# Attention with the latent heads' fifth score product and the meta keys' value product at full height

## The chip, the cores and the metric

The kernel runs on one core of a Trainium2 chip. The metric is the device time of one execution in microseconds (us). A core has TensorE (PE, matrix products, with its weight loads listed apart as PEld), VectorE (DVE), ScalarE (ACT), GpSimd (POOL) and SyncE (SP), which here issues most DMAs. Matrix products read two operands from SBUF, one held in the array (the weights) and one streamed, and add into PSUM.

## What is computed

Two transformer blocks run on 2048 tokens. The change is in the attention of the second one, which puts 16 meta tokens ahead of the 2048 (so L = 2064 keys) and has two kinds of heads:

```
q_m = concat([q[..., :NOPE_DIM], rotate(q[..., NOPE_DIM:])])        # 4 latent heads, 128 + 64 wide
k_m = concat([kv[..., :NOPE_DIM], broadcast(k_rot)])                # the 64 rotated columns are shared
o_mla = attend(q_m, k_m, v_m, QK_DIM ** -0.5)
o_gqa = attend(qg, kg, vg, GQA_DIM ** -0.5)                         # 4 grouped heads on 2 key heads, 128 wide
```

`attend` is softmax(q k^T * scale) v over all 2064 keys. The outputs of the meta queries are not needed.

## The kernel before

**Precision.** Operands of matrix products are split in two parts, high and low, each held as fp32r; a product of two split operands is made of three (high x high, high x low, low x high), added up in PSUM.

**Stages.** The kernel runs one stage after the other: first block, projections of the second (`GqaKeys.early` and `late` start loads of keys and values at the end of it), attention (`phase_d`), output projection and routing, experts. In the trace attention lies between about 1392 and 2670 us.

**Units.** Attention is 64 units, each one head and 256 queries (`QT`): 32 of the grouped heads (`hd` 4 to 7) and then 32 of the latent heads (`hd` 0 to 3). A unit has two halves `j` of 128 queries. Its steps are methods of `Unit`:

- `q(j, g)`: the scores of 128 queries against key group g (512, 400 or three times 384 keys; ten such calls in a unit). A grouped head takes three products (L1308 to L1310). A latent head takes two more for the 64 rotated columns (L1312, L1313). `qr` holds high and low part of the rotated query on top of each other, 64 partitions each; `kT[0][:, 1]` and `kT[1][:, 1]` hold the high and the low part of the rotated key, each written twice, on partitions 0 to 63 and 64 to 127. So L1312 makes (high + low query) x high key in one product, and L1313 the high query x low key on 64 partitions. After each group DVE takes the row maximum (L1314).
- `e(j, g)`: exp on ACT into `P`. After group 1 POOL copies the 16 meta columns three times beside themselves (L1329).
- `t(p)`: four transposes of `P` into PSUM (L1344), and a split by ACT (`ph`, L67) and DVE (`pl`, L68).
- `h(p)`, `l(p)`: value products with the high and low part of the weights of softmax (L1367), four and two.
- `m`, `a`: the same for the meta keys. `m` transposes four copies of the 16 columns (L1351); ACT copies them to `pm`, and DVE turns the lower 32 partitions into the low part. `a` is one value product with 64 partitions of `pm` against 64 of the value tile (`vc[0]` or `gk.v[0]`, block `NT`), where the DMAs of `META_ROWS` put high and low values in the matching order.
- `f`: the last step of a unit.

**Order.** Within attention the order is written out by hand in `ORDERS` (a latent unit plays `ORDERS[1]`): `n` is the next unit, `c` the current, `p` the previous one; `nq04` is `q(0, 4)` of the next unit, `ca` is `a` of the current. Every engine takes its part of this list in order. `ORDERS[1]` reads:

```
"nq00 ct1 ce13 nq01 ce12 ch0 pf ct2 ce14 cl0 ch1 nq02 nq03 nq04 ct3 cl1 ch2 ne02 ct4 ne01 ne00 ne03 "
"cl2 ch3 ne04 nq10 ct5 nq13 cl3 ct6 nq11 nq12 nq14 ch4 ct7 ch5 ne10 cl5 cm cl4 ne11 cl6 ch7 ch6 cl7 "
"ca nt0"
```

In `ORDERS[0]`, for grouped heads, the end is `nt0 ca cl7`. Scores have five PSUM buffers (`psS`), transposes two (`psT`), sums of values one (`psA`).

Of the kernel before, what the change touches and what calls it, by code (L numbers as in the profile page):

```python
# [8 lines left out]
F32 = mybir.dt.float32  # L9
F32R = mybir.dt.float32r  # L10
# [3 lines left out]
OP = mybir.AluOpType  # L14
# [7 lines left out]
NT = S // 128  # L22
# [782 lines left out]


def phase_c(cx, a, h, dr, mix, early, late):
    tc, nc = cx.tc, cx.nc
    es, ez, er = ExitStack(), ExitStack(), ExitStack()
# [40 lines left out]
    with es, tc.manual_schedule():  # L850
# [311 lines left out]
        t3 = cx.pool(es, "ct3")  # L1162
        pending += queries(NT - 1, t3)
        early()
        stats(NT)
        for n_, f in enumerate(pending):
# [12 lines left out]
QT = 256  # L1179
# [11 lines left out]
     "cl2 ch3 ne04 nq10 ct5 nq13 cl3 ct6 nq11 nq12 nq14 ch4 ct7 ch5 ne10 cl5 cm cl4 ne11 cl6 ch7 ch6 cl7 "  # L1191
     "ca nt0"))
META_ROWS = ((0, 32), (16, 48))


META_PART = ((S, L),)
# [3 lines left out]
def load_keys(nc, dst, src, parts=WHOLE):  # L1200
    for c0, c1 in parts:
        at = META_AT if c0 == S else c0 if c0 < META_AT else c0 + N_META
        nc.sync.dma_start(dst[:, at:at + c1 - c0].bitcast(F32), src[:, c0:c1])


class GqaKeys:
# [4 lines left out]
    def early(self):  # L1211
        nc, dr = self.cx.nc, self.dr
        c = self.cx.pool(self.es, "dg", side="right")
        self.kT = [c.tile([128, 2, L], F32R, name=f"kg{z}") for z in range(2)]
        self.v = [c.tile([128, KT, 256], F32R, name=f"vg{z}") for z in range(2)]
        self.q0 = c.tile([128, 2, QT], F32R, name="q0")
        nc.sync.dma_start(self.q0.bitcast(F32), dr["qg"][:, :, 0, :QT])
        for part in KEY_PARTS[:2]:
            for z in range(2):
                load_keys(self.cx.nc, self.kT[z][:, 0, :], self.dr["kT"][:, z, 0, :], [part])  # L1220

    def values(self, z, b):
        nc, src, bs = self.cx.nc, self.dr["v"], slice(b * 128, (b + 1) * 128)
        nc.sync.dma_start(self.v[z][:, :NT, bs].bitcast(F32), src[z, :S, bs].rearrange("(k p) d -> p k d", p=128))
        for p0 in META_ROWS[z]:
            nc.sync.dma_start(self.v[0][p0:p0 + N_META, NT, bs].bitcast(F32), src[z, S:, bs])
# [9 lines left out]


def phase_d(cx, a, dr, o, gk, after_gqa, first):
    tc, nc = cx.tc, cx.nc
    mm = nc.tensor.matmul  # L1240
    es = ExitStack()
    with es, tc.tile_pool(name="ds", bufs=5, space=PSUM) as psS, \
            tc.tile_pool(name="dp", bufs=2, space=PSUM) as psT, \
            tc.tile_pool(name="da", bufs=1, space=PSUM) as psA:
        t_ = cx.pool(es, "dt", 2)
        c = cx.pool(es, "dc")
        kT = [c.tile([128, 2, L], F32R, name=f"kT{z}") for z in range(2)]
        vc = [c.tile([128, KT, 128], F32R, name=f"vc{z}") for z in range(2)]
        wv = [c.tile([128, 4, 128], F32R, name=f"wv{z}") for z in range(2)]
        wvr = t_.tile([128, 4, 128], F32, name="wvr", bufs=1)  # L1250

        def load_k(z, b):
            load_keys(nc, kT[z][:, b, :], dr["kT"][:, z, 2 + b, :])

        def load_v(z):
            nc.sync.dma_start(vc[z][:, :NT, :].bitcast(F32), dr["c"][z, :S, :].rearrange("(k p) d -> p k d", p=128))
            for p0 in META_ROWS[z]:
                nc.sync.dma_start(vc[0][p0:p0 + N_META, NT, :].bitcast(F32), dr["c"][z, S:, :])
# [12 lines left out]
        def load_q(u):  # L1271
            qc, hd = place(u)
            ts = slice(qc * QT, (qc + 1) * QT)
            if u == 0:
                return gk.q0, None
            q = t_.tile([128, 2, QT], F32R, name="q", bufs=3)
            src = dr["qm"] if hd < 4 else dr["qg"]
            nc.sync.dma_start(q.bitcast(F32), src[:, :, hd % 4, ts])
            qr = None
            if hd < 4:  # L1280
                qr = t_.tile([128, QT], F32R, name="qr", bufs=3)
                nc.sync.dma_start(qr.bitcast(F32), dr["qr"][:, hd, ts])
            return q, qr
# [3 lines left out]
        class Unit:  # L1287
# [10 lines left out]
            def q(self, j, g, last=NG - 1):  # L1298
                if len(self.P) == j:
                    self.mx.append(cx.c.tile([128, 8], F32, name="mx", bufs=4))  # L1300
                    self.P.append(t_.tile([128, L + 3 * N_META], F32, name="P", bufs=4))
                js = slice(j * 128, (j + 1) * 128)
                kt = kT if self.mla else gk.kT
                b = 0 if self.mla else (self.hd - 4) // 2
                gs = slice(*GROUPS[g])
                po = psS.tile([128, 512], F32, name="S")[:, :gs.stop - gs.start]
                q, qr = self.qs, self.qr
                mm(po, q[:, 0, js], kt[0][:, b, gs], start=True, stop=False)  # L1308
                mm(po, q[:, 0, js], kt[1][:, b, gs], start=False, stop=False)
                mm(po, q[:, 1, js], kt[0][:, b, gs], start=False, stop=not self.mla)  # L1310
                if self.mla:
                    mm(po, qr[:, js], kT[0][:, 1, gs], start=False, stop=False)  # L1312
                    mm(po, qr[:64, js], kT[1][:64, 1, gs], start=False, stop=True)  # L1313
                nc.vector.tensor_reduce(self.mx[j][:, g:g + 1], po, AX.X, OP.max)  # L1314
                self.sg[j, g] = po
                if g == last:
                    nm = cx.c.tile([128, 1], F32, name="nm", bufs=4)
                    nc.vector.tensor_reduce(nm, self.mx[j][:, :NG], AX.X, OP.max)
                    nc.vector.tensor_scalar(nm, nm, -self.scale, None, op0=OP.mult)  # L1319
                    self.nm.append(nm)  # L1320
                    self.sm.append(cx.c.tile([128, 8], F32, name="sm", bufs=4))
# [26 lines left out]
            def m(self):  # L1348
                ps = psT.tile([128, 2, QT], F32, name="T")[:64, 0, :]
                for j in range(2):  # L1350
                    nc.tensor.transpose(ps[:, j * 128:(j + 1) * 128], self.P[j][:, META_AT:META_AT + 4 * N_META],  # L1351
                                        cx.ident)
                self.pm = t_.tile([64, QT], F32R, name="pm")
                nc.scalar.copy(self.pm, ps)
                nc.vector.tensor_tensor(self.pm[32:], ps[32:], self.pm[32:].bitcast(F32), OP.subtract)

            def val(self, k, z):
                if self.mla:
# [26 lines left out]
                    self.add(2 * p + i, 0, self.pp[p][1][:, i, :])  # L1385

            def a(self):
                self.add(NT, 0, self.pm, 64)

            def f(self):  # L1390
                ps = psT.tile([128, 2, QT], F32, name="T")
# [507 lines left out]
def phase_g(cx, a, h1, acc, tables, olist, out):  # L1899
# [4 lines left out]
    with es, tc.tile_pool(name="gp", bufs=4, space=PSUM) as pj, \  # L1904
# [23 lines left out]
        class Slot:  # L1928
# [142 lines left out]
            def down(self, cs, get, begin, end, feed):  # L2071
# [16 lines left out]
                for j in range(self.nt if early else 0):  # L2088
                    open_[j] = (pd if j < 2 else pj).tile([128, 512], F32, name="pd" if j < 2 else "pj")
                    self.product(open_[j], j, ws, range(early))  # L2090
# [345 lines left out]
def block_kernel(tc, a, out):  # L2436
    cx = Ctx(tc)
    with tc.tile_pool(name="scratch", bufs=1, space=DRAM) as dp:
        def scratch(name, shape, dt=F32):
            return dp.tile(list(shape), dt, name=name)  # L2440

        hT = scratch("hT", (128, 10, S))
        h = scratch("h", (L, D))
        dr = {"v": scratch("dr_v", (2, L, 256)), "c": scratch("dr_c", (2, L, 128)),
              "kT": scratch("dr_kT", (128, 2, 4, L)), "qg": scratch("dr_qg", (128, 2, 4, S)),
              "qm": scratch("dr_qm", (128, 2, 4, S)), "qr": scratch("dr_qr", (128, 4, S))}
        o = scratch("o", (S, D))
        h1 = scratch("h1", (ROWS, D))
        acc = scratch("acc", (ROWS, D))
        tables = [scratch(f"table{k}", (NE * STRIDE, 2)) for k in range(TOPK)]  # L2450
        olist = scratch("olist", (DUMP, 2), I32)
        mix = MixOut(cx, a, hT, h)
        phase_a(cx, a, hT, mix.ahead)
        gk = GqaKeys(cx, a, dr)
        phase_c(cx, a, h, dr, mix, gk.early, gk.late)
        op = OutProj(cx, a)
        phase_d(cx, a, dr, o, gk, op.load, partial(op.first, o))
        phase_f(cx, a, op, o, h, h1, acc, tables, out)
        phase_g(cx, a, h1, acc, tables, olist, out)
        cx.close()  # L2460
# [55 lines left out]
```

## Time and profile before

| | |
|---|---|
| runs | 5524.70, 5524.92, 5529.76 us; median 5524.92 us |
| profiled execution | span 5522.8 us from its first to its last instruction |
| busy over the span | PE 96%, weight loads 87%, DVE 68%, ACT 49%, POOL 29% |
| granted TensorE clock over the span | 0.984 of full speed |

The profile gives no time of its own for the profiled execution beside the span. The median of the runs is 2.1 us above the span. A row of the timeline has the start of an instruction (or of several alike in a row, with their number at the end) and how long it took; the time from one start to the next is what the engine needs for the first of them.

### The profile page before, as it was taken

How to read it: one execution, taken by the hardware profiler on the slowest of the kernel's cores; microseconds unless marked ns; L12 is line 12 of the kernel's file. 1: busy time of each engine (PE TensorE's matmuls, PEld its weight loads, DVE VectorE, ACT ScalarE, POOL GpSimd, SP SyncE). 2: the span in 40 equal slices, each digit the busy share in tenths (PEclk: the TensorE clock that was granted, in tenths of full speed). 3: DMA queues.
4: the chain of work that ended last, by engine and by line, in shares of the span. 5: the costliest groups of instructions: out<-in, count | busy, mean ns of one | idle time of the engine just before them, and what ended most of it. 6: DMA issues, size and time to landing. Idle time of an engine off the chain costs nothing. (4 is left out here: it accounts for less than half of the span.)

```text
span 5522.8 us, 89101 instructions
## 1 busy us (share of the span) xinstructions
PE 5316.3 (96%) x33672; PEld 4777.8 (87%) x33672; DVE 3734.1 (68%) x6827; ACT 2689.6 (49%) x5404; POOL 1605.8 (29%) x1567
## 2 busy tenths in 40 slices
PE   8999999899999999999997999999999999999997
PEld 7888878687899977777776999999999999998886
DVE  6787768544787755555697755766667667777758
ACT  4443433333677644445433544455555545555553
POOL 1232137555000021000343322233333233323327
PEclk9999999999999999999998999999999999999998
DMA  4333344344410110000335655666666666767675
GB/s 129 115 111 100 92 151 155 111 145 144 121 52 27 31 46 25 22 24 31 129 123 155 211 153 168 194 185 183 196 194 197 191 200 196 212 193 206 201 211 183
DMA packets 733017, 761.08 MB, mean 138 GB/s; under 512 B 109700, under 2 KB 673870, under 8 KB 732582
## 3 DMA queue, kind: packets, MB, share of 16 engines
q1 hardware_dynamic: 702768, 678.51, 39.3%
q0 software_dynamic: 27776, 74.33, 5.6%
q8 instruction: 267, 4.37, 0.3%
q10 hardware_dynamic: 2038, 2.48, 0.1%
q14 instruction: 168, 1.38, 0.1%
HBM read 626.35 MB, written 128.84 MB: 137 GB/s over the span
## 5 line engine op out<-in xcount | busy, mean ns | idle before, releaser
L68 DVE TENSOR_TENSOR wlo<-raw,whi 128x1024 fp32r<-128x1024 f32 (+1 forms) x751 | 923.7, 1240 | 433.1 <-ACT whi L67 423.3
L67 ACT CAST whi<-raw 128x1024 fp32r<-128x1024 f32 (+1 forms) x1000 | 960.8, 987 | 481.6 <-PE pj L73 166.2
L68 POOL TENSOR_TENSOR wlo<-raw,whi 128x1024 fp32r<-128x1024 f32 (+1 forms) x249 | 552.9, 2221 | 1705.0 <-ACT whi L67 1525.6
L72 PE MATMUL pj<-xsA,whi 128*128 128x256 f32 (+11 forms) x1792 | 593.5, 331 | 19.5 <-ACT g L2038 9.5
L73 PE MATMUL pj<-xsA,whi 128*128 128x256 f32 (+11 forms) x1792 | 590.8, 330 | 0.3 <-DVE xsA L68 0.3
L74 PE MATMUL pj<-xsA,wlo 128*128 128x256 f32 (+11 forms) x1792 | 589.3, 329 | 0.0
L67 ACT CAST ph<-T 128x512 fp32r<-128x512 f32 x512 | 300.4, 587 | 503.6 <-PE T L1344 496.9
L68 DVE TENSOR_TENSOR pl<-T,ph 128x512 fp32r<-128x512 f32 x512 | 353.5, 691 | 206.0 <-ACT ph L67 203.5
L2011 PE MATMUL pj<-xsB,whi 128*128 128x312 f32 (+11 forms) x1664 | 483.5, 360 | 4.3 <-DVE g L2041 4.3
L1314 DVE TENSOR_REDUCE mx<-S 128x1 f32<-128x384 f32 (+2 forms) x640 | 360.8, 581 | 95.1 <-PE S L1313 94.6
L2013 PE MATMUL pj<-xsB,wlo 128*128 128x156 f32 (+11 forms) x1664 | 418.2, 251 | 0.0
L72 PE MATMUL pd<-whi,atA 128*128 128x256 f32 (+4 forms) x1360 | 395.2, 291 | 17.4 <-ACT atA L67 15.0
L73 PE MATMUL pd<-wlo,atA 128*128 128x256 f32 (+4 forms) x1360 | 384.0, 282 | 8.1 <-POOL wlo L68 7.0
L74 PE MATMUL pd<-whi,atA 128*128 128x256 f32 (+4 forms) x1360 | 384.6, 283 | 3.8 <-DVE atA L68 3.5
L1325 ACT ACTIVATE P<-S,nm 128x384 f32<-128x384 f32 (+2 forms) x640 | 384.3, 609 | 7.2 <-DVE nm L1319 4.0
L1329 POOL COPY P<-P 128x48 f32<-128x48 f32 x128 | 28.5, 223 | 1176.9 <-ACT P L1325 1163.2
L72 PEld LDWEIGHTS pj<-xsA,whi 128*128 128x128 f32 x1792 | 339.7, 190 | 33.3 <-ACT g L2038 10.4
L74 PEld LDWEIGHTS pj<-xsA,wlo 128*128 128x128 f32 x1792 | 339.9, 190 | 10.7
L73 PEld LDWEIGHTS pj<-xsA,whi 128*128 128x128 f32 x1792 | 340.3, 190 | 9.7 <-DVE xsA L68 0.5
L2011 PEld LDWEIGHTS pj<-xsB,whi 128*128 128x128 f32 x1664 | 315.2, 189 | 14.8 <-DVE g L2041 4.9
L2013 PEld LDWEIGHTS pj<-xsB,wlo 128*128 128x128 f32 x1664 | 319.9, 192 | 0.2
L1344 PE MATMUL T<-ident,P 128*128 128x128 f32 x2048 | 314.6, 276 | 2.6 <-ACT P L1325 1.7
(580 smaller groups left out, 14544.2 us busy)
## 6 DMA issues: line engine op xcount, KB each, us to landing
raw<-in_w_gate_up_dram SPq DMA_DIRECT2D x256, 1024.0 KB
raw<-in_w_down_dram SPq DMA_DIRECT2D x128, 1024.0 KB
raw<-in_w_in_dram SPq DMA_DIRECT2D x120, 512.0 KB
ht<-h SPq DMA_DIRECT2D x32, 512.0 KB
xt<-in_x_dram SPq DMA_DIRECT2D x30, 512.0 KB
hT<-gt SPq DMA_DIRECT2D x20, 512.0 KB
hf<-hT SPq DMA_DIRECT2D x40, 256.0 KB
h<-xt SPq DMA_DIRECT2D x16, 512.0 KB
```

Source lines behind the costliest of these rows:

```text
L67: nc.scalar.copy(hi, src)
L68: (lo_engine or nc.vector).tensor_tensor(lo, src, hi.bitcast(F32), OP.subtract)
L72: mm(ps, w[0], x[0], start=start, stop=False)
L73: mm(ps, w[0], x[1], start=False, stop=False)
L74: mm(ps, w[1], x[0], start=False, stop=stop)
L1314: nc.vector.tensor_reduce(self.mx[j][:, g:g + 1], po, AX.X, OP.max)
L1325: nc.scalar.activation(self.P[j][:, c0:c1], self.sg.pop((j, g)), AF.Exp, bias=self.nm[j], scale=self.scale, accum_out=self.sm[j][:, g:g + 1])
L1329: nc.gpsimd.tensor_copy(meta[:, 1:, :], meta[:, :1, :].to_broadcast([128, 3, N_META]))
L1344: nc.tensor.transpose(ps[:, i, j * 128:(j + 1) * 128], self.P[j][:, k0:k0 + 128], cx.ident)
L2011: mm(ps[:, :2 * n], hi[:, k, :], self.xp[:, k, :], start=first, stop=False)
L2013: mm(ps[:, :n], lo[:, k, :], xs[:, k, 0, :], start=False, stop=last)
```

## The change

The fifth score product of a latent head reads all 128 partitions of `qr` and of `kT[1][:, 1]` in place of the first 64. The other 64 hold the low query and a second copy of the low key, so the product now adds low query x low key.

The value product of the meta keys reads 96 partitions (`META_K`) in place of 64. Partitions 64 to 95 of the value tiles and of `pm` are set to zero once, by POOL; for this `pm` becomes two tiles that live through the stage (`metas`), which the units take in turn.

```
+META_K = 96
...
+        nc.gpsimd.memset(self.v[0][64:META_K, NT, :].bitcast(F32), 0.0)
         nc.sync.dma_start(self.q0.bitcast(F32), dr["qg"][:, :, 0, :QT])
...
+        metas = [c.tile([META_K, QT], F32R, name=f"pm{i}") for i in range(2)]
+        for tl in (vc[0][64:META_K, NT, :], *[q[64:META_K] for q in metas]):
+            nc.gpsimd.memset(tl.bitcast(F32), 0.0)
...
-                    mm(po, qr[:64, js], kT[1][:64, 1, gs], start=False, stop=True)
+                    mm(po, qr[:, js], kT[1][:, 1, gs], start=False, stop=True)
...
-                self.pm = t_.tile([64, QT], F32R, name="pm")
-                nc.scalar.copy(self.pm, ps)
-                nc.vector.tensor_tensor(self.pm[32:], ps[32:], self.pm[32:].bitcast(F32), OP.subtract)
+                self.pm = metas[self.u % 2]
+                nc.scalar.copy(self.pm[:64], ps)
+                nc.vector.tensor_tensor(self.pm[32:64], ps[32:], self.pm[32:64].bitcast(F32), OP.subtract)
...
-                self.add(NT, 0, self.pm, 64)
+                self.add(NT, 0, self.pm, META_K)
```

The order on PE, ACT, DVE and SP stays as it was. On POOL four memsets come in. Before, POOL's rows at the passage from the projections (`vl`, `kf`, `rp`) to attention (`P`) are these:

```order
521 L1049 TENSOR_TENSOR vl<-kf,vh 128x128
522 L1000 TENSOR_TENSOR rs<-ss,invn 16x3
523 L78 TENSOR_SCALAR rs<-rs 16x3
...
529 L1049 TENSOR_TENSOR vl<-kf,vh 16x128
530 L1116 TENSOR_TENSOR rp<-rp,r_4_12370 128x512
531 L1329 COPY P<-P 128x48 x68
```

In the changed kernel they are these (its line numbers are up to five higher):

```order
521 L1049 TENSOR_TENSOR vl<-kf,vh 128x128
522 L1218 MEMSET vg_12228 32x256
523 L1000 TENSOR_TENSOR rs<-ss,invn 16x3
524 L78 TENSOR_SCALAR rs<-rs 16x3
...
530 L1049 TENSOR_TENSOR vl<-kf,vh 16x128
531 L1116 TENSOR_TENSOR rp<-rp,r_4_12371 128x512
532 L1334 COPY P<-P 128x48
533 L1255 MEMSET vc_12426 32x128
534 L1255 MEMSET pm_12431 32x256
535 L1255 MEMSET pm_12432 32x256
536 L1334 COPY P<-P 128x48 x67
```

One memset stands ahead of the last statistics of the projections, three between the first and the second copy of meta columns of unit 0.

## Rows read from the trace of the kernel before

**Rows 1.** Windows of grouped and latent units: length, busy PE, PEld, DVE, ACT, POOL; clock, DMA.

```profile
1420.00:1895.00 475.00, 475.00 (x3456) 453.21 (x3456) 375.63 (x872) 339.51 (x902) 13.48 (x61) 1.00 0.16 47
1945.10:2561.00 615.90, 615.90 (x3618) 481.89 (x3616) 351.01 (x779) 290.10 (x784) 58.36 (x77) 1.00 0.10 31
```

**Rows 2.** Instructions of L1313 and L1367: count, ns minimum/median/maximum, starts.

```profile
L1313 PE MATMUL S<-kT,qr x320: 435/441/498, 1896.3 to 2650.5; 64*128 64x384 f32 x128, 64*128 64x512 f32 x32
...
L1367 PE MATMUL acc<-pm,vg x32: 379/380/380, 1420.0 to 1917.5; 64*128 64x256 f32 x32
```

**Rows 3.** Timeline of PE, score groups of a latent unit, then value products.

```profile
2100.40 0.34 PE L1309 MATMUL S<-kT,q 128*128 128x384 f32 x1
...
2100.75 0.34 PE L1312 MATMUL S<-kT,qr 128*128 128x384 f32 x1
2101.02 0.44 PE L1313 MATMUL S<-kT,qr 64*128 64x384 f32 x1
2101.39 0.44 PE L1308 MATMUL S<-kT,q 128*128 128x384 f32 x1
2101.67 0.34 PE L1309 MATMUL S<-kT,q 128*128 128x384 f32 x1
...
2102.29 0.44 PE L1313 MATMUL S<-kT,qr 64*128 64x384 f32 x1
2102.66 0.74 PE L1367 MATMUL acc<-ph,vc 128*128 128x256 f32 x4
2103.24 0.60 PE L1344 MATMUL T<-ident,P 128*128 128x128 f32 x4
```

**Rows 4.** Timeline of PE: transposes behind L1313, and values and transposes elsewhere.

```profile
2108.18 0.49 PE L1313 MATMUL S<-kT,qr 64*128 64x512 f32 x1
2108.61 0.66 PE L1344 MATMUL T<-ident,P 128*128 128x128 f32 x4
2109.02 0.43 PE L1308 MATMUL S<-kT,q 128*128 128x400 f32 x1
...
2117.09 0.64 PE L1367 MATMUL acc<-ph,vc 128*128 128x256 f32 x4
2117.57 0.60 PE L1344 MATMUL T<-ident,P 128*128 128x128 f32 x4
2117.93 0.48 PE L1367 MATMUL acc<-pl,vc 128*128 128x256 f32 x2
```

**Rows 5.** Timeline of PE around the meta keys' product of two following latent units.

```profile
2106.03 0.40 PE L1367 MATMUL acc<-pl,vc 128*128 128x256 f32 x2
2106.36 0.38 PE L1367 MATMUL acc<-pm,vc 64*128 64x256 f32 x1
2106.67 0.66 PE L1344 MATMUL T<-ident,P 128*128 128x128 f32 x4
...
2130.05 0.38 PE L1367 MATMUL acc<-pm,vc 64*128 64x256 f32 x1
```

**Rows 6.** Another line with 64 rows, in the first block's cross-attention.

```profile
L388 PE MATMUL mm<-kT,qh x128: 274/279/383, 69.3 to 655.0; 64*128 64x256 f32 x128
```

**Rows 7.** Timeline of PE behind attention: a line with 96 rows.

```profile
2710.78 0.39 PE L74 MATMUL pj<-wo,ol 128*128 128x512 f32 x1
2711.01 0.62 PE L1696 MATMUL pj<-bd,gg 96*128 96x512 f32 x2
2711.47 0.40 PE L72 MATMUL pj<-wo,oh 128*128 128x512 f32 x1
2711.71 0.40 PE L73 MATMUL pj<-wo,oh 128*128 128x512 f32 x1
```

**Rows 8.** Timeline of all engines in that latent unit: three steps of other engines and PE.

```profile
2117.54 0.59 ACT L1325 ACTIVATE P<-S,nm 128x384 f32<-128x384 f32 x1
...
2118.73 0.40 PE L1308 MATMUL S<-kT,q 128*128 128x512 f32 x1
...
2129.10 0.42 DVE L1355 TENSOR_TENSOR pm<-T,pm 32x256 fp32r<-32x256 f32 x1 [0.23 <-ACT pm L1354]
```

## The prediction

> **What bounds the kernel now.** I read the windows of the attention stage first, then the two changed lines, then PE's timeline from start to start. In the windows [rows 1] PE is busy for 475.00 of 475 us while grouped heads run, and for 615.90 of 615.9 us while latent heads run. It waits for nobody: the other engines have room (DVE 375.63 and 351.01 us, ACT 339.51 and 290.10 us). So attention lasts as long as PE's list of products, and time taken out of that list comes out of the stage, up to the point at which another engine is late. What follows attention cannot start ahead of it, so the gain stays.
>
> A busy PE is not a fast one, so the second step is what a product takes. L1313 takes 441 ns in the median and the meta keys' product 380 ns [rows 2]; L1312, with as many columns as L1313, shows 0.34 us [rows 3]. The true price is the time from start to start, the third step. In [rows 3] two products of 384 columns from L1309 to L1312 take 0.35 us, so 0.175 each. L1313 then starts 0.27 after L1312, the next product 0.37 after L1313, and the one behind it 0.28 later. That is 0.095, 0.195 and 0.105 us over the usual step, 0.39 in all, and nobody is waited for. The same three steps stand around the meta keys' product, which has other operands, other columns and other neighbours [rows 5]. What the two have in common is 64 rows between neighbours of 128.
>
> Height alone is not slow: a line with 64 rows that mostly follows its own kind has a median of 279 ns for 256 columns, and only its maximum, 383, looks like the meta keys' 380 [rows 6, 2]. So the price belongs to the passage between heights, once in and once out.
>
> **What the change removes.** Of the ten score groups of a latent unit, four are followed by another score group, three by value products and three by transposes (the order as written: nq02, nq03, nq11, nq12; nq01, nq13, nq14; nq00, nq04, nq10).
> - Followed by scores: 0.39 us, above.
> - By values: from L1313 to the end of four value products 0.95 us [rows 3], where four values take 0.48 [rows 4] and the fifth product 0.175: 0.295, and 0.095 on the way in: 0.39.
> - By transposes: 0.84 us from L1313 with 512 columns to the end of four transposes [rows 4]; 512 columns take 0.23 [rows 7], four transposes 0.36 [rows 4]: 0.25, and 0.09 on the way in: 0.34.
>
> Per unit 7 x 0.39 + 3 x 0.34 = 3.75 us, in 32 units 120.0 us (320 products [rows 2]).
>
> The meta keys' product stands once in each of 64 units. In a latent unit two value products ahead of it take 0.33 us where 0.24 is usual, it itself 0.31 in place of 0.12 [rows 5, 4], and the transposes behind it lose 0.05 as above: 0.34. In a grouped unit values follow, for which I take the 0.39 of such neighbours. 32 x (0.34 + 0.39) = 23.4 us.
>
> Together 143.4 us. A latent unit now takes 23.69 us from one meta product to the next [rows 5]; it would take 23.69 - 3.75 - 0.34 = 19.60.
>
> **What it adds, and whether that hides.**
> - The full-height fifth product: the trace has its twin in L1312, same query tile, same shape, 0.175 us when a full-height product follows. Its bounds are 0.175 and the present 0.27; I take the first, since L1312 and L1310 load different weights back to back at that pace.
> - The 96-row product: bounds are no extra and the present 0.34 to 0.39. A line with 96 rows stands between full-height products [rows 7]: 0.23 us into it, 0.46 for its two, 0.24 out. Those are the usual steps of 512 columns, so I take no extra.
> - Four memsets on POOL, each of 32 partitions and at most 256 elements. 61 POOL instructions, most of them copies of 128 x 48, take 13.48 us [rows 1], 0.22 each; I put a memset at under 0.5 us (estimate). POOL's idle time covers them, 97% of the grouped window. Three stand ahead of the second copy of meta columns of unit 0 and wait until memory of the projections is free; behind them that copy, and behind the copy `cm` of unit 0 on PE. The first meta product starts at 1420.0 us [rows 2], near the end of its unit, so a delay of some us is covered; bounds 0 and 5 us, once. I take 0.
> - New waits on PE. The tightest places are two. The first exp of a half ends at 2118.13 and frees the score buffer that PE takes at 2118.73 [rows 8]: 0.60 us to spare. Between the last score group, which starts that chain, and this point lies one passage out (0.25), and the chain starts 0.10 earlier because the fifth product is that much shorter: 0.45 remain. The low meta part is ready at 2129.52 [rows 8], used at 2130.05 [rows 5]; 0.53, less 0.09: 0.44 remain. Over the whole unit (615.9 / 23.69 = 26 units in the window [rows 1]) DVE needs 13.5 us, ACT 11.2 and the weight loads 18.5 of the new 19.60: 69%, 57% and 95%. The grouped units run with 79%, 71% and 95% [rows 1] and PE has no wait there. So I allow 1.5 us for waits in all.
>
> Sum: 5522.8 - 143.4 + 1.5 = 5380.9 us for the span; the median of the runs is 2.1 us above the span, so 5383 us.
>
> **The rivals.**
> - *New waits eat part of it* (0.09). Speaks for it: the buffers of scores and transposes were in step with the slower list, and 0.44 us is not much. Against: the two spares above and the grouped units. If every latent unit lost 0.5 us: 16 us, 5399; if half of the gain went: 5455.
> - *96 rows are treated as 64 are* (0.03): 23.4 us stay, 5406. [rows 7] speak against it.
> - *The full-height weights cannot be loaded under the product before* (0.03). Then the fifth product's load lies bare, as the load of 64 rows seems to now; the way in and out keeps its 0.29 and only the third step goes: 32 x (7 x 0.10 + 3 x 0.05 + 0.10 + 0.05) = 32 us, 5493. Against it speaks the 0.175 us from L1309 over L1310 to L1312, each with its own weights at full height [rows 3]. The Trainium skill, "TensorE: Matmul & The Clock Gate", Part 3 ("What overlaps and what doesn't"), says that a weight load overlaps a running product only where their row groups differ; by that rule this rival would hold. The trace does not agree with it, by that 0.175.
> - *The change does nothing* (0.02): 5525, if the steps came from something else than height, such as late operands. Against it: L1312 reads the same query tile without delay, and the profile names nobody waited for. The same page of the Trainium skill, "Why this matters for your kernels", has it that one product with few rows takes as long as one with 128; by that rule alone nothing is won. [rows 6] agree with it for products among their kind, and [rows 3] show what it leaves out.
> - *Slower* (0.02): the denser list makes the chip take TensorE to its lower level, 1.2 in place of 2.4 GHz. A product then takes up to twice as long; the latent units, 32 x 19.60 = 627 us, would have to spend 143 / 627 = 23% of their time there to give everything back, and with a third of it the time would be 5592. Against it: the granted clock was 1.00 all through the grouped units, which are as dense [rows 1].
>
> **How the numbers follow.** The forecast, 5383 us, has a chance of 0.81. Its own spread: the rows are rounded to 0.01 us, which is some 3 us over 320 products; runs of before lie up to 5 us apart; waits from 0 to 8 us. That makes 5374 to 5392. The first rival in its milder half reaches 5402; with it the range holds some 85%, and the others lie outside. No change within 0.2% is 11 us, about what a measurement of this kernel can tell. Faster: 0.81 + 0.09 + 0.03 + 0.03 = 0.96; within it 0.02; slower 0.02.
>
> **What the profile after would show.** the fifth product with the shape 128*128 and near 338 ns like L1312; steps of 0.175 through all five products; meta products near 283 ns; latent units 19.6 us apart and grouped ones 0.39 less than now; PE still busy all the time in both windows. I would be wrong if PE shows waits for exp or for `pl` in latent units, if meta products stay at 380 ns, or if the steps of 0.27 and 0.37 remain with the full shape.

## The result and the profile after

The changed kernel takes 5382.5 us (median; 5381.6 to 5385.3) beside 5524.8 us of the kernel before on the same chip: a ratio of 0.9738, 95% interval 0.9726 to 0.9750. That is 142.3 us less; the forecast was 5383 us, 141.9 less. The profiled execution has a span of 5381.2 us, with a granted clock of 0.983.

The windows of grouped and of latent units, which answer to [rows 1] (length, busy PE, PEld, DVE, ACT, POOL, then clock and DMA):

```profile
1423.00:1903.00 480.00, 480.00 (x3571) 466.81 (x3570) 387.76 (x897) 344.04 (x928) 13.90 (x62) 1.00 0.16 48
1924.20:2425.00 500.80, 500.80 (x3559) 486.43 (x3558) 337.43 (x767) 286.37 (x769) 61.62 (x75) 1.00 0.13 38
```

PE is still busy all the time in both, at full clock; in the latent window DVE now has 67%, ACT 57% and the weight loads 97%. So nothing took the place of what was removed. The two changed lines, to be read beside [rows 2] (count, ns minimum/median/maximum, first and last start):

```profile
L1318 PE MATMUL S<-kT,qr x320: 332/336/398, 1887.7 to 2512.4; 128*128 128x384 f32 x128, 128*128 128x512 f32 x32
...
L1372 PE MATMUL acc<-pm,vg x32: 364/366/368, 1423.1 to 1905.0; 96*128 96x256 f32 x32
...
L1372 PE MATMUL acc<-pm,vc x32: 283/285/285, 1924.2 to 2527.6; 96*128 96x256 f32 x32
```

The fifth score product (now L1318) has 336 ns where it had 441. The timeline of PE, with the stretches that answer to [rows 3 to 5]:

```profile
2100.05 0.40 PE L1372 MATMUL acc<-pl,vc 128*128 128x256 f32 x2
2100.28 0.28 PE L1372 MATMUL acc<-pm,vc 96*128 96x256 f32 x1
2100.41 0.60 PE L1349 MATMUL T<-ident,P 128*128 128x128 f32 x4
2100.76 0.48 PE L1313 MATMUL S<-kT,q 128*128 128x512 f32 x1
...
2106.12 0.34 PE L1317 MATMUL S<-kT,qr 128*128 128x384 f32 x1
2106.31 0.33 PE L1318 MATMUL S<-kT,qr 128*128 128x384 f32 x1
2106.48 0.34 PE L1313 MATMUL S<-kT,q 128*128 128x384 f32 x1
2106.65 0.33 PE L1314 MATMUL S<-kT,q 128*128 128x384 f32 x1
...
2111.45 0.40 PE L1318 MATMUL S<-kT,qr 128*128 128x512 f32 x1
2111.69 0.60 PE L1349 MATMUL T<-ident,P 128*128 128x128 f32 x4
2112.04 0.42 PE L1313 MATMUL S<-kT,q 128*128 128x384 f32 x1
...
2119.85 0.28 PE L1372 MATMUL acc<-pm,vc 96*128 96x256 f32 x1
```

The steps around the fifth product are 0.19, 0.17 and 0.17 us, where they were 0.27, 0.37 and 0.28. From it to the end of four transposes it takes 0.59 in place of 0.84. Around the meta product there stand 0.23, 0.13 and 0.35 us for what took 0.33, 0.31 and 0.42. From one meta product to the next, 2100.28 to 2119.85, a latent unit takes 19.57 us; it took 23.69 [rows 5]. The 0.42 ran from 2106.67 [rows 5] to this row of the kernel before:

```profile
2107.09 0.47 PE L1308 MATMUL S<-kT,q 128*128 128x512 f32 x1
```

### The profile page after: what moved, and what is told of

It reads as the page before. It is cut to its first block, busy times and chain, and to the rows that moved or that the text cites. A ratio compares the mean times of both kernels' runs of the same rounds, so it can differ in the third digit from the quotient of the medians.

```text
span 5381.2 us, 89111 instructions
## 1 busy us (share of the span) xinstructions
PE 5179.1 (96%) x33672; PEld 4795.2 (89%) x33672; DVE 3721.3 (69%) x6827; ACT 2690.7 (50%) x5404; POOL 1607.1 (30%) x1571
## 5 line engine op out<-in xcount | busy, mean ns | idle before, releaser
L72 PE MATMUL pj<-xh,whi 128*128 128x512 f32 (+1 forms) x784 | 314.2, 401 | 3.7 <-ACT whi L67 3.7
```

What stands on the lines that cost most here:

```text
L72: mm(ps, w[0], x[0], start=start, stop=False)
```

## The experiments

The theory: a passage of the array between products of 64 rows (half height) and products of more has a price, in and out, whatever the products do. The rivals: each half-height product is dear by itself; its weight load lies bare, which means that it does not run beneath the product before; 96 rows count as 64 do; the memsets cost something.

For all runs I compare the stretch from the first meta product (the meta keys' value product) of the grouped units to the last one of the latent units, read from the rows of the value products with `pm`. Before, it went from 1420.0 [rows 2] to 2666.3 us, 1246.3 us long; the second row, of the latent units, is this:

```profile
L1367 PE MATMUL acc<-pm,vc x32: 379/379/379, 1940.6 to 2666.3; 64*128 64x256 f32 x32
```

In the changed kernel it goes from 1423.1 to 2527.6 (rows above): 1104.5 us, 141.8 less. This stretch is the same to 0.1 us in the one pair of kernels that differ in nothing on PE (the kernel before and the fourth run), while whole runs differ by some us.

**The fifth score product alone.**

```
-                    mm(po, qr[:64, js], kT[1][:64, 1, gs], start=False, stop=True)
+                    mm(po, qr[:, js], kT[1][:, 1, gs], start=False, stop=True)
```

> The kernel before with the fifth score product alone at full height; the meta keys' product keeps its 64 rows. Theory (the price is the passage between 64 and 128 rows, 0.39 or 0.34 us each): 320 passages go, 120.0 us, so 5404.8 us; the meta products keep 380 ns, and the five score products step by 0.175 us. If the two edits depend on each other (one passage hides behind the other's), the sum of this and of the other edit alone misses the 142.3 us that both together gave by more than 8 us.

It took 5409.6 us beside 5523.9 of the kernel before on the same chip: 0.9787 (0.9770 to 0.9803). Its meta products:

```profile
L1367 PE MATMUL acc<-pm,vg x32: 379/380/380, 1424.2 to 1918.0; 64*128 64x256 f32 x32
L1367 PE MATMUL acc<-pm,vc x32: 379/379/379, 1937.4 to 2551.5; 64*128 64x256 f32 x32
```

The stretch is 1127.3 us, 119.0 less than before, where 120.0 was expected. This trace also has the 1.6 us of new waits that the changed kernel has (see the waits below: 2.4 us in two waits, 0.8 in one before), so the passages alone gave some 120.6. The meta products are as dear as before.

**The meta product alone.**

```
-                    mm(po, qr[:, js], kT[1][:, 1, gs], start=False, stop=True)
+                    mm(po, qr[:64, js], kT[1][:64, 1, gs], start=False, stop=True)
```

(of the changed kernel)

> The changed kernel with the fifth score product back at 64 rows; the meta keys' product has 96. Theory: 64 passages go, 23.4 us, so 5501.4 us. Rival (96 rows are treated as 64 are): 5524.8 us, and 0.27 and 0.37 us around the meta product as before.

It took 5502.0 us: 0.9956 (0.9939 to 0.9972). Its meta products:

```profile
L1372 PE MATMUL acc<-pm,vg x32: 364/366/368, 1424.1 to 1909.7; 96*128 96x256 f32 x32
L1372 PE MATMUL acc<-pm,vc x32: 282/283/283, 1932.5 to 2648.0; 96*128 96x256 f32 x32
```

The stretch is 1223.9 us, 22.4 less. So 96 rows are not treated as 64 are, and the two edits add up: 119.0 + 22.4 = 141.4 beside 141.8 for both.

**Half height twice.**

```
-                    mm(po, qr[:64, js], kT[1][:64, 1, gs], start=False, stop=True)
+                    mm(po, qr[:64, js], kT[1][:64, 1, gs], start=False, stop=False)
+                    mm(po, qr[:64, js], kT[1][:64, 1, gs], start=False, stop=True)
```

> The kernel before with the fifth score product issued twice in a row at 64 rows (the high query x low key part is added twice). Theory (a passage costs, a half-height product beside its kind does not): only the columns come on top, 192 x 0.175 + 64 x 0.182 + 64 x 0.23 = 60 us, so 5585 us. Rival (each half-height product costs its 0.34 to 0.39 us extra by itself): 60 + 120 = 180 us, 5705 us. Rival (the weight load of each half-height product lies bare, 0.09 us): 60 + 29 = 89 us, 5614 us.

It took 5584.3 us, 1.0105 (1.0088 to 1.0122), which is 60.5 us more. The stretch goes from 1428.5 to 2733.8 us, 1305.3 long, 59.0 more. Its timeline on PE (L1313 and L1314 are the two half-height products):

```profile
2100.19 0.34 PE L1312 MATMUL S<-kT,qr 128*128 128x384 f32 x1
2100.46 0.44 PE L1313 MATMUL S<-kT,qr 64*128 64x384 f32 x1
2100.74 0.34 PE L1314 MATMUL S<-kT,qr 64*128 64x384 f32 x1
2101.01 0.44 PE L1308 MATMUL S<-kT,q 128*128 128x384 f32 x1
2101.28 0.34 PE L1309 MATMUL S<-kT,q 128*128 128x384 f32 x1
2101.46 0.34 PE L1310 MATMUL S<-kT,q 128*128 128x384 f32 x1
```

The second half-height product takes 0.34 us, as a full-height one does, and lengthens the group by its columns alone: 320 more of them cost 59 us, not 180 and not 89. Both rivals that put the price on the product fall.

The steps are 0.27, 0.28, 0.27, 0.27, then 0.18. Over the usual 0.175 that is about 0.10 four times. So one passage has two parts: 0.10 us ahead of the first product of the new height, and as much between that one and the second. Where a single half-height product stands alone, the second part of the way in and the first of the way out fall into one step, the 0.37 of [rows 3].

**The memsets alone.** The changed kernel with both products at 64 rows:

```
-                self.add(NT, 0, self.pm, META_K)
+                self.add(NT, 0, self.pm[:64], 64)
```

and the fifth product as in the kernel before.

> The changed kernel with both products back at 64 rows, so that only the four memsets and the two lasting tiles for the meta weights are left of it. Theory: 5524.8 us, within 5. Rival (the memsets hold up the first units, by the first meta product at 1423.1 us in place of 1420.0): 3 us more, and the first meta product at 1423 us again.

It took 5525.4 us, 1.0002 (0.9992 to 1.0011). The meta products, and POOL's timeline at the start of attention:

```profile
L1372 PE MATMUL acc<-pm,vg x32: 379/380/380, 1422.9 to 1920.3; 64*128 64x256 f32 x32
L1372 PE MATMUL acc<-pm,vc x32: 379/379/379, 1943.4 to 2669.2; 64*128 64x256 f32 x32
```

```profile
1399.19 0.22 POOL L1334 COPY P<-P 128x48 f32<-128x48 f32 x1 [9.07 <-ACT P L1330]
1401.05 0.20 POOL L1255 MEMSET vc<- 32x128 f32 x1 [1.64 <-DMA dr_qr<-ol]
1401.19 0.55 POOL L1255 MEMSET pm<- 32x256 f32 x2
1405.82 0.23 POOL L1334 COPY P<-P 128x48 f32<-128x48 f32 x1 [4.07 <-issue]
```

The stretch is 1246.3 us, to the tenth that of before. The three memsets take 0.75 us and are done four us ahead of the copy behind them. The rival's row is there (first meta product at 1422.9 in place of 1420.0), but it is not theirs: the first run, without any memset, has it at 1424.2, and the third, without any too, at 1428.5. The stage starts at different places from run to run.

**The fifth product at 96 rows**, in the changed kernel.

```
-                    mm(po, qr[:, js], kT[1][:, 1, gs], start=False, stop=True)
+                    mm(po, qr[:96, js], kT[1][:96, 1, gs], start=False, stop=True)
```

> The changed kernel with the fifth score product at 96 rows (32 of its 64 low query x low key rows are left out). Theory (up to 64 rows the array works in another height than above; 96 counts as full): same as the changed kernel, 5382.5 us, steps of 0.175 us. Rival (any change of the number of rows between neighbours costs): 5502 us.

It took 5387.8 us beside 5525.9: 0.9753 (0.9736 to 0.9769). Its timeline on PE:

```profile
2111.05 0.34 PE L1317 MATMUL S<-kT,qr 128*128 128x384 f32 x1
2111.23 0.34 PE L1318 MATMUL S<-kT,qr 96*128 96x384 f32 x1
2111.41 0.34 PE L1313 MATMUL S<-kT,q 128*128 128x384 f32 x1
2111.59 0.34 PE L1314 MATMUL S<-kT,q 128*128 128x384 f32 x1
```

Steps of 0.18 us: between 96 and 128 rows no passage is paid, and 320 products at 96 rows are nearly as good as at 128. The stretch (1427.1 to 2534.2) is 1107.1 us, 2.6 more than with 128 rows, some 0.01 us for each of 320 products. This is no scatter, since it recurs in every unit; three meta products that follow each other:

```profile
L1372 PE MATMUL acc<-pm,vc x3: 286/286/286, 2105.2 to 2144.5; 96*128 96x256 f32 x3
```

Two latent units take 39.3 us, 19.65 each, where the changed kernel takes 19.57. What the small difference is, stays open.

**Side by side.** The kernel before; in nq03 and nq12 the half-height product comes first:

```
+                ahead = self.mla and (j, g) in ((0, 3), (1, 2))
+                if ahead:
+                    mm(po, qr[:64, js], kT[1][:64, 1, gs], start=True, stop=False)
-                mm(po, q[:, 0, js], kt[0][:, b, gs], start=True, stop=False)
+                mm(po, q[:, 0, js], kt[0][:, b, gs], start=not ahead, stop=False)
...
-                    mm(po, qr[:, js], kT[0][:, 1, gs], start=False, stop=False)
-                    mm(po, qr[:64, js], kT[1][:64, 1, gs], start=False, stop=True)
+                    mm(po, qr[:, js], kT[0][:, 1, gs], start=False, stop=ahead)
+                    if not ahead:
+                        mm(po, qr[:64, js], kT[1][:64, 1, gs], start=False, stop=True)
```

> The kernel before, all heights as they were; in two of the ten score groups of a latent unit (nq03 and nq12) the half-height product comes first in place of last, so that it stands beside the one of the group ahead of it. Two of the ten passages in and out of a unit fall together with their neighbours'. Theory: 32 x 2 x 0.39 = 25 us less, 5499.8 us, without a product or a row changed. Rival (the price belongs to each half-height product): 5524.8 us.

It took 5502.6 us, 0.9961 (0.9948 to 0.9973). The meeting of the two on PE (L1317 ends a group, L1310 begins the next, L1311 is the next group's first full-height product), and its meta products:

```profile
2111.90 0.34 PE L1315 MATMUL S<-kT,qr 128*128 128x384 f32 x1
2112.16 0.44 PE L1317 MATMUL S<-kT,qr 64*128 64x384 f32 x1
2112.44 0.34 PE L1310 MATMUL S<-kT,qr 64*128 64x384 f32 x1
2112.71 0.44 PE L1311 MATMUL S<-kT,q 128*128 128x384 f32 x1
...
2113.34 0.34 PE L1315 MATMUL S<-kT,qr 128*128 128x384 f32 x1
2113.52 0.33 PE L1311 MATMUL S<-kT,q 128*128 128x384 f32 x1
```

```profile
L1371 PE MATMUL acc<-pm,vg x32: 379/380/380, 1425.5 to 1922.6; 64*128 64x256 f32 x32
L1371 PE MATMUL acc<-pm,vc x32: 379/379/379, 1944.9 to 2646.7; 64*128 64x256 f32 x32
```

The stretch is 1221.2 us, 25.1 less than before, for two pairs of passages saved in each of 32 units: 0.39 us for a pair. Not a product and not a row was changed; only the neighbours were.

No run pointed to a version that beats the changed kernel: it leaves no product of up to 64 rows in the units.

## Why the prediction was right

- *PE's list bounds the stage, and what is taken out of it is won.* So it was: both windows after have PE busy all the time.
- *0.39 and 0.34 us per passage pair, 120.0 and 23.4 us.* Measured 119.0 (first run, some 120.6 without its new waits) and 22.4 (second). The latent unit came out at 19.57 us where 19.60 was forecast. (The three parts that I named for the meta product of a latent unit add up to 0.33 as written; the transposes behind it took 0.42 in place of 0.36, so 0.06, which makes the 0.34 that I used.)
- *The price belongs to the passage between heights.* Shown from two sides: more half-height products without more passages cost their columns alone (third run), and fewer passages with the same products give 0.39 us for each pair (sixth run).
- *96 rows as good as 128.* Shown by the second and the fifth run, up to some 0.01 us for each product in the fifth. *Memsets at nothing*: the fourth run finds no cost, to within about 6 us of the whole run (its interval), and its rows have three of them done four us ahead of the next work on POOL.
- *Full-height weights load under the product before.* The rival that they cannot falls with the steps of 0.17 to 0.19 us around L1318. The rule of the Trainium skill that stood with it ("TensorE: Matmul & The Clock Gate", Part 3, a weight load overlaps a running product only where row groups differ) is not what these rows show: all five products of a group now have all rows, and none waits for its load.
- *1.5 us for new waits.* The steady units have none. In two of the last units, where the output projection's first block is prepared in between, PE waits for DVE behind `f`; after and before:

```profile
2438.78 0.66 PE L1349 MATMUL T<-ident,P 128*128 128x128 f32 x4 [1.57 <-DVE pl L68]
...
2459.36 0.66 PE L1349 MATMUL T<-ident,P 128*128 128x128 f32 x4 [0.81 <-DVE pl L68]
```

```profile
2562.51 0.66 PE L1344 MATMUL T<-ident,P 128*128 128x128 f32 x4 [0.82 <-DVE pl L68]
```

The first of the two stands in the same unit as the one before, and has grown from 0.82 to 1.57 us; the second, one unit later, is new. Together 1.56 us came on top. DVE itself had waited 2.40 us for `ph` from ACT there, which was busy with squares for the output projection (L1488). I had allowed for the size, but looked for it at the score buffers and at `pm`, not there. I had also named PE waits for `pl` in latent units as a sign of being wrong: they are there, and that sign was drawn too tight, because the sum had a term for them.

Outside this stretch the two executions differ by little: attention's first meta product is 3.1 us later after the change, and from the last one to the end of the span it is 2853.6 in place of 2856.5 us. The experiments show shifts of that size without any of the change's edits, so I read nothing into them; that they cancel is luck.

A second sign that I had named was wrong. I expected meta products near 283 ns everywhere; in grouped units they show 364 to 368 ns, because transposes stand ahead of them there. The price is gone all the same: from the first to the last meta product of the grouped units it is 485.6 us in the second run and 497.5 in the kernel before [rows 2]. That is 11.9 us less in 31 units, 0.38 for each, where 0.39 was forecast.

A duration of a product depends on what stands ahead of it; the step from start to start, summed over a few products, is what counts.

## What to carry to other kernels

On a stage that PE bounds, look at the steps from start to start wherever products of 64 rows stand between products of more: a pair of passages took 0.34 to 0.39 us here, twice the 0.175 us of the product itself, and none of it shows as a wait of PE. Pad such an operand with zeros, or with rows that are there anyway and do no harm, to 96 or 128 rows, or else put the products of small height beside each other, so that they share one passage. Heights under 64, and between 64 and 96, were not run.

## What I had not expected

A passage is paid in two parts, about 0.10 us ahead of the first product of the new height and 0.10 ahead of the second (third run: 0.27, 0.28, 0.27, 0.27 where 0.175 is usual). In the kernel before, the step of 0.37 us behind L1313 looked like one large wait, but it holds the second part of the way in and the first of the way out.

The rows of the weight loads (PEld) show more of a passage, and they hold a sign to look for. Before:

```profile
2113.01 0.34 PE L1310 MATMUL S<-kT,q 128*128 128x384 f32 x1
2113.01 0.19 PEld L1312 LDWEIGHTS S<-kT,qr 128*128 128x128 f32 x1
...
2113.19 0.34 PE L1312 MATMUL S<-kT,qr 128*128 128x384 f32 x1
...
2113.45 0.18 PEld L1313 LDWEIGHTS S<-kT,qr 64*128 64x128 f32 x1 [0.25 <-issue]
2113.46 0.44 PE L1313 MATMUL S<-kT,qr 64*128 64x384 f32 x1
```

The load for L1312 starts with the product ahead of it, L1310. The load for L1313 starts only with its own product, after 0.25 us of idle time for which the profile names nobody ("issue"). So at this passage the load does not run beneath the product before. In the latent window of the kernel before ([rows 1]) the waits are listed like this (us in total, times, longest):

```profile
PEld S L1313 <- issue: 71.5, 260, 0.4
...
PEld S L1308 <- issue: 19.5, 104, 0.2
PEld T L1344 <- issue: 17.3, 78, 0.2
PEld acc L1367 <- issue: 14.7, 78, 0.2
```

These are the ways in and out of 260 fifth score products, 26 units' worth; after the change the list of the latent window has no such line. The latent units' meta products are not on the list although they paid too, so the steps from start to start decide. What the array does during a passage no run shows.
